# Two-layer decoder step on one core: more short products of ones ahead of the first block, the first norm's squares in another place and width, the end in two halves of tokens

## The chip, the core and the metric

The kernel runs on one core of a Trainium2 chip. A core has five engines with a queue of instructions each, and work on one waits for work on another by semaphores: TensorE (PE: matrix products, with a separate row PEld for loading weights), VectorE (DVE: elementwise work), ScalarE (ACT: elementwise functions with a scale), GpSimd (POOL: elementwise, and slower) and SyncE (SP: here it issues nearly all transfers between device memory and the on-chip memory). Sixteen DMA engines carry the transfers. Products land in PSUM, a small memory of banks from which DVE and ACT read.

The metric is the device time of one execution in microseconds. Before the change it is 601.29 us, the median of 3 runs (601.08 to 602.26). A separate execution was profiled; its time and span stand in the table below.

## The reference, cut to what matters

264 columns of tokens (256 of a prompt and 8 single tokens of a sample group) pass two layers of width 1024, a mixer and a feed-forward net each, and a final norm:

```python
def rmsnorm(x, g):
    xf = x.astype(jnp.float32)
    y = xf * lax.rsqrt(jnp.mean(xf * xf, axis=-1, keepdims=True) + EPS)
    return (y * g).astype(x.dtype)

def moba_gmlp_mixer(x, pos, past_kv, norm_g, w_in, sgu_gain, sgu_w, sgu_b, w_out):   # layer 0
    h = rmsnorm(x, norm_g)
    z = h @ w_in
    q, k, v, bu, bv = jnp.split(z, [...], axis=-1)
    ...                                   # rotary positions, attention, a gated mixer
    return x + y, new_kv, bvn
...
xp, cp = conv_ffn(xp, conv_zero, ffn_norm[layer], ...)      # after each mixer
y_prompt = rmsnorm(xp, final_norm)
y_sample = rmsnorm(xs, final_norm)
```

Two things of it matter here: the very first `rmsnorm` with the product `h @ w_in` behind it, and the very last `rmsnorm`, whose result is the output `y`.

## The kernel before, in words

**Layout.** The residual stream lies transposed: channels on the 128 partitions (eight groups `m` of 128), 264 tokens along the free dimension. A weight matrix is cut into blocks of 128x128; a block is one step of `run`, and eight blocks are a tile of weights. To keep float32 accuracy each weight tile and each operand is split into a high and a low part: ACT copies the high part (`wh`, `xg_h`), DVE subtracts it from the source (`wl`, `xg_l`), and a block is three products of PE: high x high, high x low, low x high (the order on PE is `xg_h,wh`, `xg_l,wh`, `xg_h,wl`). All of PE's products carry line L215 in the profile, since a helper issues them; they are told apart by the tiles' names.

**Blocks and tiles of the first product.** Layer 0's input product has 160 blocks. Blocks 0 to 19 run over the channel groups k = 0 to 4 with four outputs inside (the four parts of `bv`); blocks 20 to 31 finish these four with k = 5 to 7; from block 32 on each output takes eight blocks in a row (q, k, bu, v). Tile t is blocks 8t to 8t+7. Tiles 0 and 1 and the input x come in six packed transfers `xw`; tiles 2 to 5 in one transfer each (`raw2` to `raw5`, 512 KB), from `raw6` on two tiles to a transfer (1 MB; `raw6` holds tiles 6 and 7).

**The first norm.** The norm's factor R is one number per token, so the kernel multiplies x by the gain only and divides later: the products start before R is known, and R is applied where a result leaves PSUM (`in0_evac`). R needs the sum of the squares over all channels: ACT squares each of the eight groups (`Norm.add`, L399), POOL adds them up one by one (L408, L411), two products with a matrix of ones (`ns_n`, float32, each in two passes) add over partitions, and ACT takes Ln and Exp (L431, L432). Up to that point the results of blocks 0 to 31 are held in four PSUM banks. Then DVE computes the tables `rope` (L657 to L659) and evacuates `bv` (L695), q and k (L687 to L693). The first use of q and k on PE is the attention product `S` of the first two heads.

**What sets the order.** Early instructions are pinned with `tc.keep_in_program_order`; the rest of the queues is laid out by a scheduler when the program is built. `run` walks over the blocks; hooks (`blk(b, f)`) insert other work on PE after b blocks, and from the first hook on PE's order is the program's. Before: `blk(30, norm0)`, `blk(82, s_qk, 0)`, `blk(108, gm_var)`. SP's queue is in order: transfers, and between them reads of the page table into registers (`page_regs`, L340). Buffers come from pools; a pool called `up` has 24 slots of one size, taken in turn, and a new tile waits until its slot's last owner is done.

**Ahead of the first product** PE runs `WARM` = 12 products of a matrix of ones (256 columns, bf16) whose result nobody reads.

**The end.** The last matrix product adds its eight outputs into X (`residual(..., operand=False)`): DVE adds (L598), ACT squares (L399), POOL sums, ACT multiplies X by the final gain (L603). The last group's squares go into the sum as a second product of ones. After Ln and Exp, DVE multiplies X by R in five pieces of 1, 2, 2, 2 and 1 channel groups (`YD`, L1109), and SP and ACT in turn send each piece out (L1110).

Of the kernel before, what the change touches and what calls it, by code (L numbers as in the profile page):

```python
# [34 lines left out]

MMB = 4
KQ = 5
WARM = 12
YD = ((0, 1), (1, 3), (3, 5), (5, 7), (7, 8))

NEG = -1e30
SCALE = HD ** -0.5
# [108 lines left out]
def _consts():  # L151
# [41 lines left out]
    ("sguw", (P, 512)), ("sgub", (P, 512)), ("poolw", (P, 512)),  # L193
]
_OUTS = [
    ("y", (KD, P, T)), ("k0", (P, 4, T)), ("v0", (P, 4, T)), ("bvn", (P, 4, NS)),
    ("k1", (P, 4, T)), ("v1", (P, 4, T)), ("poolp", (P, 4, NST)), ("pools", (P, 4, NS, 16)),
    ("cv0", (P, NF, 10)), ("cv1", (P, NF, 10)), ("cs0", (P, NF, NS)), ("cs1", (P, NF, NS)),
]
# [3 lines left out]
def tile_decoder_step(ctx: ExitStack, tc: tile.TileContext, a):  # L203
# [36 lines left out]
    def at(name):  # L240
        return psa.tile([P, 512], F32, tag="at", name=name)
# [45 lines left out]

    LOOK = 3
    pos = [0]

    def split(t):
        for tt in range(len(splits), min(t + (2 if t == 3 else LOOK), NT - 1) + 1):
            ci = chunk_of[tt]
            for c in range(ci, min(ci + 3, len(_CHUNKS))):
                raw(c)
            o = (tt * 8 - coff[ci]) * P
            src = raws[ci][:, o:o + 8 * P]
            h, l = splits[tt] = wtiles(tt)
            s.activation(h, src, AF.Copy)  # L299
            v.tensor_tensor(l, src, h.bitcast(F32), ALU.subtract)  # L300
        return splits[t]

    spare = (32, 40)
# [65 lines left out]
    warm = con.tile([P, 256], BF16, name="warm")  # L369
    tc.keep_in_program_order(v.memset(warm, 1.0))  # L370
    pw = at("warm")
    for i in range(WARM):
        tc.keep_in_program_order(pe.matmul(pw[:, :256], warm[:, :P], warm, start=i == 0, stop=i == WARM - 1))

    ident = cst("ident")
    ones = con.tile([P, P], F32, name="ones")
# [13 lines left out]
            tc.keep_in_program_order(j)  # L390

    class Norm:
        def __init__(self, name, two=False):
            self.name, self.two, self.last = name, two, []
            self.acc = None

        def add(self, m, src=None):
            q = sm.tile([P, T], F32, tag="sq", name=f"sq_{self.name}{m}")
            i = s.activation(q, X[:, m, :] if src is None else src, AF.Square)  # L399
            if src is not None:  # L400
                tc.keep_in_program_order(i)
            if m == KD - 1 and self.two:
                self.last.append(q)
            elif self.acc is None:
                self.acc = q
            elif m == 1:
                n = sm.tile([P, T], F32, tag="acc", name=f"acc_{self.name}", bufs=2)
                g.tensor_tensor(n, self.acc, q, ALU.add)  # L408
                self.acc = n
            else:  # L410
                g.tensor_tensor(self.acc, self.acc, q, ALU.add)  # L411

        def finish(self, pin=False):
            return rstd_of([self.acc] + self.last, 1.0 / D, self.name, pin)
# [6 lines left out]
        def finish2(self):  # L421
# [127 lines left out]
    def ffn(l, xg, nrm, down_evac, hooks=None):  # L549
        cw, cb = vec("cw"), vec("cb")  # L550
        wc = lambda i, j: cw[:, (l * 3 + i) * NF + j:(l * 3 + i) * NF + j + 1]
        cvo = sm.tile([P, NF, 10], F32, tag="cvo", name=f"cvo{l}", bufs=1)
        act = [mv(f"a{l}_{i}") for i in range((NF + 3) // 4)]
        half = {}
        R = None
        nrm.split()

        def norm():
            nonlocal R
            R = nrm.finish2()  # L560
# [31 lines left out]
    def residual(gain, name, operand=True):  # L592
        xg = [mv(f"xg_{name}{i}") for i in range(2)] if operand else None
        nrm = Norm(name, not operand)

        def evac(m, o):
            m = m[1]
            v.tensor_tensor(X[:, m, :], X[:, m, :], o, ALU.add)  # L598
            if operand:
                operand_tile(xg[m // 4], m, X[:, m, :], gain[:, m:m + 1])  # L600
            nrm.add(m)
            if not operand:
                s.activation(X[:, m, :], X[:, m, :], AF.Copy, scale=gain[:, m:m + 1])  # L603
        return xg, nrm, evac

    def pick(xg):
        return lambda m, k: hl(xg, k)
# [3 lines left out]


    xg = [mv(f"xg_0{i}") for i in range(2)]
    nrm = Norm("n0", True)
    for tt in range(2):
        splits[tt] = wtiles(tt)

# [19 lines left out]
    for m in range(1, 5):  # L637
        part(m, s)()
        operand_tile(xg[m // 4], m, xin[m], GAIN[:, m:m + 1], pin=True)
        if m != 2:  # L640
            nrm.add((m - 1) // 2 if m < 4 else 2, xin[(m - 1) // 2 if m < 4 else 2])
    whole(2)
    for m in range(5, KD):
        operand_tile(xg[m // 4], m, xin[m], GAIN[:, m:m + 1], pin=True)
    for m in range(3, KD):
        nrm.add(m, xin[m])
        if m == 4:
            whole(3)
        elif m == 6:
            whole(4)  # L650
    rope = f4("rope")
    R0, held = [], []

    def norm0():
        R = nrm.finish(pin=True)
        R0.append(R)
        v.tensor_tensor(rope[:, 0, :], CS[:, 0, :], R, ALU.mult)  # L657
        v.scalar_tensor_tensor(rope[:, 2, :], CS[:, 1, :], SCALE, R, ALU.mult, ALU.mult)
# [285 lines left out]
    st1 = {}  # L944

    qz1 = sample_z("l1")

    def norm1():
        nonlocal R
        R = nrm1.finish2()  # L950
        sigmoid_set()

    edge = f4("edge", (P, 384))
# [150 lines left out]
    _, nrm, evac = residual(vec("fin"), "fin", operand=False)  # L1104
    ffn(1, xg, norm_f, evac)
    R = nrm.finish()
    for i, (m, e) in enumerate(YD):
        x = X[:, m:e, :]
        v.tensor_tensor(x, x, R.unsqueeze(1).to_broadcast([P, e - m, T]), ALU.mult)  # L1109
        (s if i % 2 else nc.sync).dma_start(a["y"][m:e].rearrange("m p t -> p m t"), x)  # L1110


def _lay(inp):
# [66 lines left out]
```

## Time and profile before

| what | before |
|---|---|
| device time, median of 3 runs | 601.29 us (601.08 to 602.26) |
| device time of the profiled execution | 602.49 us |
| span of the profiled execution | 600.7 us |
| PE busy | 588.6 us, 98% of the span |
| DVE busy | 422.9 us, 70% |
| ACT busy | 343.3 us, 57% |
| POOL busy | 107.9 us, 18% |
| first and last block product starts on PE | 5.08 us, 591.30 us |

A row of the timeline reads: start in us from the span's start, duration in us, engine, line, operation, what is written <- what is read, shape, count; in brackets how long the engine was idle before and what it waited for. Rows with a count above one merge neighbours of the same kind. In the table of windows each engine has its busy time in the stretch. The profiled execution took 1.8 us more than its span. PE is busy nearly all the time, so the places where it is not, at both ends and in between, are few and can be listed.

### The profile page before, as it was taken

The page shows a single profiled execution, that of the slowest core. Times are in us where ns is not written, and L with a number is a line of the kernel's source. Part 1 is how long each engine was busy: PE and PEld are TensorE (multiplying, and loading weights), DVE is VectorE, ACT ScalarE, POOL GpSimd, SP SyncE. Part 2 cuts the span into 40 slices and gives each one's busy share as a digit, 9 for nine tenths or more (in the row PEclk, how much of TensorE's full clock was granted, in tenths as well). Part 3 has the DMA queues.
Part 4 walks back from the last instruction along what each step waited for, and adds up shares of the span by engine and source line. Part 5 has one row for each costly group of instructions (what it writes and reads, how often), then busy time and mean ns, then how long its engine had stood idle before and what let it go on. Part 6 is the DMA issues. An engine that isn't in the chain of part 4 may idle for free.

```text
span 600.7 us, 12394 instructions
## 1 busy us (share of the span) xinstructions
PE 588.6 (98%) x4900; PEld 569.6 (95%) x4900; DVE 422.9 (70%) x733; ACT 343.3 (57%) x600; POOL 107.9 (18%) x103
## 2 busy tenths in 40 slices
PE   8999999999999999999999999999999999999994
PEld 6988879999999999999999879999999999999994
DVE  7899565977778777665559676687777777864432
ACT  7657754675655656644454466657656565564441
POOL 4100002303222232210120000031232323211110
PEclk9999999999999999999999999999999999999998
DMA  8998835454555545795467763554545454555402
GB/s 319 337 399 323 316 121 202 152 201 152 200 170 182 186 165 202 264 378 214 155 247 256 261 203 113 174 204 148 201 154 206 147 205 159 193 187 202 181 1 74
DMA packets 28092, 122.42 MB, mean 204 GB/s; under 512 B 3330, under 2 KB 5250, under 8 KB 16642
## 3 DMA queue, kind: packets, MB, share of 16 engines
q1 hardware_dynamic: 27200, 120.42, 56.1%
q10 hardware_dynamic: 834, 1.20, 0.6%
q8 instruction: 39, 0.64, 0.4%
q14 instruction: 19, 0.16, 0.1%
HBM read 117.65 MB, written 3.96 MB: 202 GB/s over the span
## 4 chain that ended last, share of the span: by engine, by line
PE 92%; DVE 3%; DMA 2%; SPq 1%; issue 1%; ACT 0%; ACTq 0%; DVEq 0%
PE mm L215 85%; DMA raw<-in_w 1%; PE pv_l L215 1%; PE sc L215 1%; DVE wl L300 1%; PE pav L215 1%; PE pt L218 1%; DMA PT<-in_pt 1%; PE S L215 1%; SPq L340 1%; PE Z L215 1%; PE pf L215 0%; DVE X L1109 0%; PE pm L215 0%; DVE rz_q L687 0%
## 5 line engine op out<-in xcount | busy, mean ns | idle before, releaser
L300 DVE TENSOR_TENSOR wl<-raw,wh 128x1024 fp32r<-128x1024 f32 x179 | 218.9, 1224 | 78.1 <-ACT wh L299 77.9
L299 ACT ACTIVATE wh<-raw 128x1024 fp32r<-128x1024 f32 x179 | 188.6, 1055 | 92.7 <-PE mm L215 84.1
L215 PE MATMUL mm<-xg_f_h,wh 128*128 128x264 f32 x704 | 200.1, 284 | 0.0
L215 PE MATMUL mm<-xg_f_l,wh 128*128 128x264 f32 x704 | 199.9, 284 | 0.0
L215 PE MATMUL mm<-xg_f_h,wl 128*128 128x264 f32 x704 | 198.6, 282 | 0.0
L215 PEld LDWEIGHTS mm<-xg_f_l,wh 128*128 128x128 f32 x704 | 132.3, 188 | 0.0
L215 PEld LDWEIGHTS mm<-xg_f_h,wh 128*128 128x128 f32 x704 | 132.2, 188 | 0.0
L215 PEld LDWEIGHTS mm<-xg_f_h,wl 128*128 128x128 f32 x704 | 132.2, 188 | 0.0
L582 POOL TENSOR_TENSOR wk<-wk 128x264 f32<-128x264 f32 x44 | 66.5, 1513 | 193.9 <-DVE wk L581 159.3
L215 PE MATMUL mm<-a_h,wh 128*128 128x264 f32 x352 | 100.1, 284 | 0.0
L215 PE MATMUL mm<-a_l,wh 128*128 128x264 f32 x352 | 99.9, 284 | 0.0
L215 PE MATMUL mm<-a_h,wl 128*128 128x264 f32 x352 | 99.4, 282 | 0.0
L215 PEld LDWEIGHTS mm<-a_l,wh 128*128 128x128 f32 x352 | 66.1, 188 | 0.0
L215 PEld LDWEIGHTS mm<-a_h,wh 128*128 128x128 f32 x352 | 66.1, 188 | 0.0
L215 PEld LDWEIGHTS mm<-a_h,wl 128*128 128x128 f32 x352 | 66.1, 188 | 0.0
L442 ACT ACTIVATE a_h<-wk 128x264 fp32r<-128x264 f32 x44 | 18.7, 424 | 73.3 <-POOL wk L582 73.3
L215 PE MATMUL mm<-xg_h,wh 128*128 128x264 f32 x160 | 47.5, 297 | 1.1 <-ACT xg_h L386 1.1
L443 DVE TENSOR_TENSOR a_l<-wk,a_h 128x264 fp32r<-128x264 f32 x44 | 19.2, 437 | 41.5 <-ACT a_h L442 41.5
L215 PE MATMUL mm<-xg_h,wl 128*128 128x264 f32 x160 | 45.7, 285 | 0.7 <-DVE wl L632 0.6
L215 PE MATMUL mm<-xg_l,wh 128*128 128x264 f32 x160 | 45.6, 285 | 0.1
L215 PE MATMUL mm<-xg_n_h,wh 128*128 128x264 f32 x128 | 38.4, 300 | 0.0
L215 PE MATMUL mm<-xg_n_l,wh 128*128 128x264 f32 x128 | 36.3, 283 | 0.0
(245 smaller groups left out, 897.3 us busy)
## 6 DMA issues: line engine op xcount, KB each, us to landing
raw<-in_w SPq DMA_DIRECT2D x89, 1024.0 KB, 4.8
K<-in_kt SPq DMA_DIRECT2D x32, 256.0 KB, 6.7
V<-in_vp SPq DMA_DIRECT2D x32, 256.0 KB, 5.2
raw<-in_w SPq DMA_DIRECT2D x4, 512.0 KB, 5.7
X<-in_x SPq DMA_DIRECT2D x4, 264.0 KB, 6.4
xw<-in_xw SPq DMA_DIRECT2D x2, 388.0 KB, 5.5
out_k<-k SPq DMA_DIRECT2D x1, 528.0 KB
out_v<-v SPq DMA_DIRECT2D x1, 528.0 KB, 5.0
```

Source lines behind the costliest of these rows:

```text
L215: return self.keep(nc.tensor.matmul(*x, **k))
L218: return self.keep(nc.tensor.transpose(*x, **k))
L299: s.activation(h, src, AF.Copy)
L300: v.tensor_tensor(l, src, h.bitcast(F32), ALU.subtract)
L340: regs.append(nc.sync.value_load(PT[0:1, i:i + 1], min_val=0, max_val=NPHYS - 1))
L442: s.activation(h, src, AF.Copy)
L443: v.tensor_tensor(l, src, h.bitcast(F32), ALU.subtract)
L582: g.tensor_tensor(A, A, C, ALU.mult)
```

## The change

Five edits:

1. `WARM` goes from 12 to 18 products, and one more of 128 columns (`busy(128)`) stands inside block 0, between its second and third product.
2. The first norm's squares leave their places among the first splits. ACT now squares groups 0 to 3 after the split of tile 3 and groups 4 and 5 to 7 (the latter three in one instruction, 128x792) after that of tile 4. POOL adds the first four (128x528, then 128x264), DVE adds the other four the same way and then both sums (`sum0`). One product of ones takes the place of two. The hook moves from block 30 to block 34, and so behind the splits of tiles 5, 6 and 7.
3. SP issues `raw6` before the reads of the page table and before `CST`; `VEC` moves to a hook at block 64.
4. Hooks further on move: `s_qk` from blocks 82 and 95 to 86 and 97, `gm_var` from 108 to 113.
5. The end works on two halves of 132 tokens: the last group is added and squared in halves, the product of ones over it and Ln and Exp are done per half, DVE writes two new tiles `y0` and `y1` (seven instructions instead of five; the last channel group takes its gain there, so ACT's L603 falls away for it), and five transfers of 4+4 and 4+2+2 groups send them out. `y` in device memory becomes (2, 128, 8, 132); the host transposes it.

```diff
-WARM = 12
-YD = ((0, 1), (1, 3), (3, 5), (5, 7), (7, 8))
+WARM = 18
+TH = T // 2
...
             pe.matmul(o, h[:, c:c + P], xl, start=False, stop=False)
+            if i == 0:
+                busy(128)
             pe.matmul(o, l[:, c:c + P], xh, start=False, stop=left[m] == 0)
...
     raw(5)
+    raw(6)
     page_regs(4)
     late(CST, a["cst"])
-    raw(6)
-    page_regs(4)
-    late(VEC, a["vec"])
-    page_regs(4)
+    page_regs(8)
...
-        if m != 2:
-            nrm.add((m - 1) // 2 if m < 4 else 2, xin[(m - 1) // 2 if m < 4 else 2])
     whole(2)
...
-    for m in range(3, KD):
-        nrm.add(m, xin[m])
-        if m == 4:
-            whole(3)
-        elif m == 6:
-            whole(4)
+    whole(3)
+    sq0 = [f4(f"sq0_{i}") for i in range(2)]
+    def sum0(e, q):
+        keep(e.tensor_tensor(q[:, 0:2, :], q[:, 0:2, :], q[:, 2:4, :], ALU.add))
+        keep(e.tensor_tensor(q[:, 0, :], q[:, 0, :], q[:, 1, :], ALU.add))
+    for m in range(4):
+        keep(s.activation(sq0[0][:, m, :], xin[m], AF.Square))
+    sum0(g, sq0[0])
+    whole(4)
+    keep(s.activation(sq0[1][:, 0, :], xin[4], AF.Square))
+    keep(s.activation(sq0[1][:, 1:4, :], first[5][2], AF.Square))
+    sum0(v, sq0[1])
+    summed = keep(v.tensor_tensor(sq0[1][:, 0, :], sq0[0][:, 0, :], sq0[1][:, 0, :], ALU.add))
...
-        R = nrm.finish(pin=True)
+        R = rstd_of([sq0[1][:, 0, :]], 1.0 / D, "n0", True)
...
-    blk(30, norm0)
+    blk(34, norm0)
+    blk(64, late, VEC, a["vec"])
-    for t, b in enumerate((82, 95, 108, 121)):
+    for t, b in enumerate((86, 97, 108, 121)):
         blk(b, s_qk, t)
-    blk(108, gm_var)
+    blk(113, gm_var)
...
+            for c in halves_:
+                keep(v.tensor_tensor(X[:, m, c], X[:, m, c], o[:, c], ALU.add))
+                keep(s.activation(sq[:, c], X[:, m, c], AF.Square))
+        def rest():
+            keep(pe.matmul(p[:, :T], ones, nrm.acc, start=True, stop=False, skip_group_check=True))
+            for c in halves_:
+                keep(pe.matmul(p[:, c], ones, sq[:, c], start=False, stop=True, skip_group_check=True))
+            ...
+            for i, c in enumerate(halves_):
+                Y = f4(f"y{i}", (P, KD, TH))
+                cuts = ((0, 4), (4, 8)) if i == 0 else ((0, 4), (4, 6), (6, 8))
+                for n, (m, e) in enumerate(cuts):
+                    w = min(e, KD - 1)
+                    keep(v.tensor_tensor(Y[:, m:w, :], X[:, m:w, c], R[:, c].unsqueeze(1).to_broadcast([P, w - m, TH]), ALU.mult))
+                    if e == KD:
+                        keep(v.scalar_tensor_tensor(Y[:, w, :], X[:, w, c], gain[:, w:w + 1], R[:, c], ALU.mult, ALU.mult))
+                    (s if n % 2 else nc.sync).dma_start(a["y"][i][:, m:e, :], Y[:, m:e, :])
```

In `split`, two hints of order to the scheduler are added: tile 5's low part behind the last sum, and a hint for tiles below 8 that are split after R, of which there are none with the hook at block 34.

More of the change, by code (lines that the diff above doesn't have):

```diff
@@ L289, in tile_decoder_step @@
     pos = [0]
+    R0 = []
     def split(t):
@@ L298, in split @@
             h, l = splits[tt] = wtiles(tt)
-            s.activation(h, src, AF.Copy)
-            v.tensor_tensor(l, src, h.bitcast(F32), ALU.subtract)
+            i = s.activation(h, src, AF.Copy)
+            if R0 and tt < 8:
+                behind(i, last[0])
+            i = v.tensor_tensor(l, src, h.bitcast(F32), ALU.subtract)
+            if tt == 5:
+                behind(i, summed)
         return splits[t]
@@ L371, in tile_decoder_step, with busy @@
     pw = at("warm")
+    def busy(n):
+        tc.keep_in_program_order(pe.matmul(pw[:, :n], warm[:, :P], warm[:, :n], start=True, stop=True))
     for i in range(WARM):
-        tc.keep_in_program_order(pe.matmul(pw[:, :256], warm[:, :P], warm, start=i == 0, stop=i == WARM - 1))
+        busy(256)
     ident = cst("ident")
@@ L392, in tile_decoder_step, with __init__, add @@
     class Norm:
[L393 to L397, printed above, removed]
+        def __init__(self, name):
+            self.name, self.acc = name, None
+        def add(self, m):
             q = sm.tile([P, T], F32, tag="sq", name=f"sq_{self.name}{m}")
[L399 to L404, printed above, removed]
+            s.activation(q, X[:, m, :], AF.Square)
+            if self.acc is None:
                 self.acc = q
@@ L411, in add @@
                 g.tensor_tensor(self.acc, self.acc, q, ALU.add)
-        def finish(self, pin=False):
-            return rstd_of([self.acc] + self.last, 1.0 / D, self.name, pin)
         def split(self):
@@ L419, in split, with finish @@
             halves(*self.hl, self.acc)
-        def finish2(self):
+        def finish(self):
             return rstd_of(self.hl, 1.0 / D, self.name, w=onesr)
@@ L559, in norm @@
             nonlocal R
-            R = nrm.finish2()
+            R = nrm.finish()
             gelu_set()
@@ L590, in ffn, with residual @@
         run(orders[f"dn{l}"], lambda m, k: hl(act, k), down_evac, hooks)
-    def residual(gain, name, operand=True):
-        xg = [mv(f"xg_{name}{i}") for i in range(2)] if operand else None
-        nrm = Norm(name, not operand)
+    def residual(gain, name):
+        xg = [mv(f"xg_{name}{i}") for i in range(2)]
+        nrm = Norm(name)
         def evac(m, o):
@@ L598, in evac, with final, rstd @@
             v.tensor_tensor(X[:, m, :], X[:, m, :], o, ALU.add)
-            if operand:
-                operand_tile(xg[m // 4], m, X[:, m, :], gain[:, m:m + 1])
+            operand_tile(xg[m // 4], m, X[:, m, :], gain[:, m:m + 1])
             nrm.add(m)
-            if not operand:
-                s.activation(X[:, m, :], X[:, m, :], AF.Copy, scale=gain[:, m:m + 1])
-        return xg, nrm, evac
+        return xg, nrm, evac
+    def final():
+        nrm = Norm("fin")
+        gain = vec("fin")
+        halves_ = [slice(0, TH), slice(TH, T)]
+        sq = sm.tile([P, T], F32, tag="R", name="sq_last", bufs=2)
+        keep = tc.keep_in_program_order
+        def evac(m, o):
+            m = m[1]
+            if m < KD - 1:
+                v.tensor_tensor(X[:, m, :], X[:, m, :], o, ALU.add)
+                nrm.add(m)
+                s.activation(X[:, m, :], X[:, m, :], AF.Copy, scale=gain[:, m:m + 1])
+                return
+            for c in halves_:
+                keep(v.tensor_tensor(X[:, m, c], X[:, m, c], o[:, c], ALU.add))
+                keep(s.activation(sq[:, c], X[:, m, c], AF.Square))
+        def rest():
+            p = at("ns_fin")
+            R = sm.tile([P, T], F32, tag="R", name="R_fin", bufs=2)
+            keep(pe.matmul(p[:, :T], ones, nrm.acc, start=True, stop=False, skip_group_check=True))
+            for c in halves_:
+                keep(pe.matmul(p[:, c], ones, sq[:, c], start=False, stop=True, skip_group_check=True))
+            def rstd(c):
+                keep(s.activation(R[:, c], p[:, c], AF.Ln, bias=epst, scale=1.0 / D))
+                keep(s.activation(R[:, c], R[:, c], AF.Exp, scale=-0.5))
+            for c in halves_:
+                rstd(c)
+            for i, c in enumerate(halves_):
[7 more added lines that the diff above has]
+                    (s if n % 2 else nc.sync).dma_start(a["y"][i][:, m:e, :], Y[:, m:e, :])
+        return evac, rest
@@ L946, in tile_decoder_step @@
     qz1 = sample_z("l1")
+    R = None
     def norm1():
         nonlocal R
-        R = nrm1.finish2()
+        R = nrm1.finish()
         sigmoid_set()
@@ L1103, in tile_decoder_step @@
     norm_f = nrm
-    _, nrm, evac = residual(vec("fin"), "fin", operand=False)
+    evac, rest = final()
     ffn(1, xg, norm_f, evac)
[L1106 to L1110, printed above, removed]
+    rest()
 def _lay(inp):
@@ L1159 @@
     o = {n: np.asarray(r.results[0]["out_" + n]) for n, _ in _OUTS}
-    y = o["y"].transpose(2, 0, 1).reshape(T, D)
+    y = o["y"].transpose(0, 3, 2, 1).reshape(T, D)
     def kv(k, w):
```

6 lines of the change are left out of this document (3 added, 3 removed).

## The prediction

> **What bounds the kernel now.** I read the page's busy line, the list of what PE waited for, and then the timeline at both ends.
>
> ```profile
> span 600.7 us, 12394 instructions
> PE 588.6 (98%) x4900; PEld 569.6 (95%) x4900; DVE 422.9 (70%) x733; ACT 343.3 (57%) x600; POOL 107.9 (18%) x103
> PE mm L215 <- ACT xg_h L386: 1.1, 1, 1.1
> PE mm L215 <- DVE wl L632: 0.6, 1, 0.6
> ```
>
> PE is the bound from 40 us to the last product; there it has no wait at all. Gains can come only from the first 40 us and from what follows the last product. The list counts only waits of half a microsecond and more, so I price PE by the times at which blocks start. Of the rows below, 7.94 is the first product of block 5, 18.32 the first norm product (30 blocks done), 19.57 the first of block 31, 38.11 the first mask product of S (82 blocks done).
>
> ```profile
> 1.20 2.74 PE L215 MATMUL warm<-warm 128*128 128x256 bf16 x12 [1.20 <-DVE warm L370]
> 5.08 0.39 PE L215 MATMUL mm<-xg_h,wh 128*128 128x264 f32 x1 [1.15 <-ACT xg_h L386]
> 5.61 0.19 PEld L215 LDWEIGHTS mm<-xg_l,wh 128*128 128x128 f32 x1 [0.34 <-DVE xg_l L387]
> ...
> 7.72 0.39 PE L215 MATMUL mm<-xg_h,wl 128*128 128x264 f32 x1
> 7.94 0.28 PE L215 MATMUL mm<-xg_h,wh 128*128 128x264 f32 x1
> ...
> 18.32 0.61 PE L215 MATMUL ns_n<-acc_n,ones 128*128 128x264 f32 x2
> ...
> 19.57 0.29 PE L215 MATMUL mm<-xg_h,wh 128*128 128x264 f32 x1
> ...
> 38.11 0.39 PE L215 MATMUL S<-maskb,identb 128*128 128x256 bf16 x2
> 39.49 0.93 PE L215 MATMUL S<-k,q 64*128 64x128 f32 x8 [0.99 <-DVE k L693]
> ```
>
> Blocks 31 to 81 take 18.54 us, 0.3635 each, with no stall. Blocks 5 to 29 would take 9.09 at that pace and took 10.38: **1.29 us lost** to waits for DVE. From 18.32 to 19.57 lie one block and the two norm products: 0.89, so 0.445 a product. S's two mask products take 0.22 (the second runs 0.11 behind the first), so 38.33 was due and 39.49 came: **1.16 lost**.
>
> Why DVE is late:
>
> ```profile
> 8.59 0.48 DVE L387 SCALAR_TENSOR_TENSOR xg_l<-xw,xw,xg_h 128x264 fp32r<-128x264 f32 x1
> 10.16 0.98 DVE L387 SCALAR_TENSOR_TENSOR xg_l<-xw,xw,xg_h 128x264 fp32r<-128x264 f32 x1
> 12.20 2.30 DVE L387 SCALAR_TENSOR_TENSOR xg_l<-xw,xw,xg_h 128x264 fp32r<-128x264 f32 x3
> 14.43 3.47 DVE L632 TENSOR_TENSOR wl<-raw,wh 128x1024 fp32r<-128x1024 f32 x2
> 17.82 1.21 DVE L300 TENSOR_TENSOR wl<-raw,wh 128x1024 fp32r<-128x1024 f32 x1
> 9.98 0.87 POOL L411 TENSOR_TENSOR acc_n<-acc_n,sq_n 128x264 f32<-128x264 f32 x1 [0.29 <-ACT sq_n L399]
> 12.46 4.35 POOL L411 TENSOR_TENSOR acc_n<-acc_n,sq_n 128x264 f32<-128x264 f32 x4 [1.61 <-ACT sq_n L399]
> ```
>
> The same `xg_l` takes 0.48 alone and 0.98 beside a POOL add; `wl` 1.21 alone and about 1.77 beside one. Over these rows that is about 2.5 us of DVE time.
>
> The chain of waits up to the tables `rope`:
>
> ```profile
> 12.82 7.99 DMA raw<-in_w
> 20.91 1.06 ACT L299 ACTIVATE wh<-raw 128x1024 fp32r<-128x1024 f32 x1 [4.50 <-DMA raw<-in_w]
> 22.37 0.43 ACT L432 ACTIVATE R_n<-R_n 128x264 f32<-128x264 f32 x1
> 23.15 0.43 DVE L657 TENSOR_TENSOR rope<-ropecs,R_n 128x264 f32<-128x264 f32 x1
> 39.01 0.43 DVE L693 TENSOR_TENSOR k<-k,rz_k 128x264 f32<-128x264 f32 x1
> ```
>
> R's sum was ready near 19.3, but on ACT's queue Ln stands behind tile 6's split, which waited for `raw6` until 20.9. From 23.15 to 39.44 DVE works without a gap, and its `k` is what S waits for.
>
> **The change, part by part.**
>
> *Products of ones.* Twelve took 2.74, 0.22 apart, so six more end near 5.2, at most 0.15 after PE's first block could start. Block 0's second product waits 0.34 for `xg_l` anyway and its third for `wl`; the 128-column product (0.06 to 0.11) fits before the third. Cost 0, between +0.3 (all of it on the path) and -0.3 (the clock is up sooner). If that cover were gone, it would be 0.15.
>
> *Squares on ACT.* The next start behind each row gives ACT's pace: an `xg_h` 0.41, a square 0.31, a split 0.95.
>
> ```profile
> 10.69 1.32 ACT L386 ACTIVATE xg_h<-xw,xw 128x264 fp32r<-128x264 f32 x3
> 11.91 0.72 ACT L399 ACTIVATE sq_n<-xw 128x264 f32<-128x264 f32 x2
> 12.53 1.05 ACT L631 ACTIVATE wh<-raw 128x1024 fp32r<-128x1024 f32 x1
> 13.48 0.72 ACT L399 ACTIVATE sq_n<-xw 128x264 f32<-128x264 f32 x2
> ```
>
> Tile 2's split began at 9.74, behind two squares that no transfer hid; now it starts at about 9.1 and tile 3's at 11.35. Four squares run from 12.3 to 13.55, tile 4's split to 14.5, the squares of groups 4 to 7 to 15.6 (the wide one 0.75, by its width between a square and a split), tile 5's split to 16.5.
>
> *Sums.* POOL now starts at 13.6 instead of before 9.98, so DVE runs undisturbed until then: tile 2's `wl` ends by 11.4, the three `xg_l` by 12.6, tile 3's `wl` by 13.7. PE, unstalled, asks for them at block 16 (11.94), block 20 (13.4) and block 24 (14.85). All 1.29 us go. Next comes tile 4's `wl` at 14.55: even at 1.77 it is done by 16.35, and block 32 is at 17.75. DVE's three adds (0.62, 0.35, 0.35 by its 528- and 264-column rows below) end near 17.7. That is new work on DVE and the thinnest place: the norm product is due at 18.48 (block 34). Tile 5's `wl` then ends by 18.9, wanted at 21.1 (block 40).
>
> The Trainium skill, page "SBUF — State Buffer", section "Who interferes with whom", says that DVE with two inputs in this memory and a reading GpSimd instruction exclude each other for the whole instruction. The rows agree that beside POOL an instruction is longer by half of one of POOL's. By that rule they would take turns: POOL's wide add to 15.5 (twice its 0.87 and more), `wl` to 16.7, POOL's second to 17.6, DVE's adds to 18.9, and PE would wait 0.45: an estimate, and the forecast would be 598.4.
>
> *One norm product instead of two*: 0.445 less on PE.
>
> *`raw6` earlier.* SP issues it behind `raw5` (9.70 + 0.43) instead of at 12.82:
>
> ```profile
> 9.70 0.43 SPq L274 DMA_DIRECT2D raw<-in_w  x1
> 18.17 0.33 SPq L274 DMA_DIRECT2D raw<-in_w  x1
> DMA to landing us min/median/max: 4.9/7.1/9.0
> ```
>
> By the `raw` transfers of the first 45 us it lands between 15.0 and 19.1; I take 17.7, near the median. Tile 6's split then ends at 18.75, tile 7's at 19.7 (PE frees its buffer at block 32), Exp at 20.7. DVE has `wl` of tiles 6 and 7 to 21.15, then `rope`: 2.0 sooner than 23.15, with tile 7 (1.14, which stood between `bv` and q) already done. `CST`, passed by 1 MB, lands some 3 us later than it would, before the masks need it at 21. The next `raw`, at 18.17, moves by less than 0.4, since SP's sixteen reads stay. `VEC` is wanted at block 130 and costs nothing at block 64.
>
> *S at block 86.* Its `k` is ready at 21.15 + (39.44 - 23.15) - 1.14 = 36.3. PE reaches block 86 at 7.94 + 81 x 0.3635 + 0.445 = 37.83, and S proper at 38.05. No wait; 1.16 goes, with 1.7 us to spare. With `raw6` at 19.1 `rope` would come at 22.4 and S would still not wait. The banks of `bv` are the other limit: block 48 (24.0) takes the first one, emptied some 1.45 after `rope` begins, at 22.6.
>
> *Hooks.* Moved work is the same work. `gm_var` comes at block 113 instead of 108; 17 blocks, 6.2 us at 0.3635, stay for its chain before block 130, where its result is wanted. I cost this at nothing; each microsecond that the chain lacks would cost one.
>
> Early sum: 1.29 + 0.445 + 1.16 = **2.89 us**.
>
> *The end.*
>
> ```profile
> 591.62 0.43 DVE L598 TENSOR_TENSOR X<-X,mm 128x264 f32<-128x264 f32 x1 [7.56 <-PE mm L215]
> 594.33 2.63 DVE L1109 TENSOR_TENSOR X<-X,R_fin 128x264 f32<-128x264 f32 x5 [2.29 <-ACT R_fin L432]
> L1109 DVE TENSOR_TENSOR X<-X,R_fin 128x528 f32<-128x528 f32 x3 | 1.9, 700 | 0.0
> L1109 DVE TENSOR_TENSOR X<-X,R_fin 128x264 f32<-128x264 f32 x2 | 0.9, 430 | 2.3 <-ACT R_fin L432 2.3
> 597.50:598.50 1.00, 0.00 (x0) 0.50 1.04 362
> 8.00:10.00 2.00, 1.00 1.04 414
> ```
>
> From the add to DVE's first multiplication: 2.71 us. In the built program the second Ln has no wait of its own, so the first waits for the products of both halves. The second half of the add ends 0.08 later (one more seam), its square, Ln and Exp each lose about 0.1 (between none and half of some 0.42), the product 0.22: 2.27, or 0.44 sooner. DVE's seven pieces: 1.02 ns a column from the two rows, so 0.70 + 0.565 + 0.295 + 0.70 + 0.43 + 2 x 0.295 = 3.28, less six seams of 0.083 = 2.78 against 2.63. The last transfer is issued 0.29 sooner, the first, twice as large, 0.17 sooner. The DMA engines are full at 362 GB/s (the windows show it); pieces with twice the bytes in a row could go at up to 414, another 0.5. I take 0.4, between 0.17 and 0.8.
>
> Sum: 2.89 + 0.4 = 3.3 us. Against the profiled execution 602.49 - 3.3 = 599.2; the median of the runs shown is 1.2 lower, so **598.0 us**.
>
> **The rivals.**
> - *R is late all the same.* If `raw6` still lands at 20.9, Ln stands behind two splits and `rope` comes at 23.85; block 48 waits for its bank until 25.25, 1.25 us. Gain 2.0: 599.3. For it: a transfer's landing is not set by its issue alone, 12.82 took 7.99. Against: none took over 9.0.
> - *DVE stays the bound.* If POOL is not what stretches DVE, 1.8 of the 2.5 us fall before tile 3's `wl`, which PE then awaits for about 0.9, and the rest makes the norm product some 0.5 late. Gain 2.89 - 1.4 + 0.4 = 1.9: 599.4, and past 600.1 if the new adds are stretched too. The rows with and without a POOL add speak against it.
> - *The clock comes up later.* The ones ran 0.22 apart and the mask products, as wide, 0.11: PE began at half speed. If it stayed there through blocks 1 to 4, twelve products would take 0.12 longer each, 1.4, of which block 4 hides some 0.2, since its product at 7.72 waits that long already: 599.2. The Trainium skill, page "TensorE: Matmul & The Clock Gate", section "What's actually happening", gives a free-running window of about 3.4 us that must be busy; six more products fill it, so by that rule the change makes this rarer.
> - *Slower.*
>
> ```profile
> 50.51 0.35 SPq L896 DMA_DIRECT2D out_k<-k  x1
> 63.17 0.82 PE L218 MATMUL pt<-CST,p 128*128 128x128 f32 x6
> ```
>
> Two new tiles shift the turn of `up`: the transposes' copy of heads 2 and 3 now takes the slot of `k`, which the transfer `out_k` reads (issued at 50.51). PE needs that copy at block 129 (the second row), 2.89 sooner than before: 60.3. At 9.0 to landing the copy is done at 60.4; each microsecond beyond costs one, and only from 13.7 on is the kernel slower by 0.2%. No transfer shown takes that long: 602.6.
>
> **How the numbers follow.** Forecast 0.70 (own range 597.2 to 598.6), late R 0.10, DVE 0.08, clock 0.06, slower 0.06. The range 597.0 to 599.9 takes in the bounds of the end and all but the last case and the worse half of DVE's. About 0.2%, 1.2 us, can be told from no change, so faster means under 600.1: 0.88; the same 0.06 (half of the DVE case, and milder forms of the last); slower 0.06.
>
> **What would show it.** Right: `xg_l` near 0.48 and `wl` near 1.21 before 14 us, no PE wait at L632, the norm product near 18.5, `rope` near 21.2, S without a wait near 38, the last group's add some 2.9 us earlier than 591.62, and about 8.7 us from it to the end of the span instead of 9.1. Wrong: a PE wait for `sq` at the norm product, for `bv` at block 48, or for `k` at S.

## The result, and the profile after

| what | before | after |
|---|---|---|
| device time, median of 6 executions each | 601.39 us (601.08 to 602.62) | 599.26 us (598.98 to 599.47) |
| ratio | | 0.9956, 95% interval 0.9945 to 0.9967 |
| device time of the profiled execution | 602.49 us | 599.23 us |
| span of the profiled execution | 600.7 us | 597.2 us |

The kernel became faster by 2.1 us, 0.44%. The forecast was 598.0 (597.0 to 599.9), 3.3 us of gain: the direction and the range held, the gain forecast was half as large again as the one measured, and the narrower range that the prediction gave its own case (597.2 to 598.6) was missed. The two profiled executions, however, lie 3.26 apart.

The page's busy line and PE's timeline of the changed kernel; the columns are those of the prediction's rows:

```profile
span 597.2 us, 12397 instructions
PE 588.4 (99%) x4907; PEld 570.4 (96%) x4907; DVE 423.4 (71%) x739; ACT 342.5 (57%) x600; POOL 104.8 (18%) x99
```

```profile
1.20 4.02 PE L215 MATMUL warm<-warm 128*128 128x256 bf16 x18 [1.20 <-DVE warm L375]
4.87 0.47 PE L215 MATMUL mm<-xg_h,wh 128*128 128x264 f32 x1
...
7.63 0.39 PE L215 MATMUL mm<-xg_h,wl 128*128 128x264 f32 x1 [0.21 <-DVE wl L666]
7.86 0.28 PE L215 MATMUL mm<-xg_h,wh 128*128 128x264 f32 x1
...
18.39 0.61 PE L215 MATMUL ns_n<-sq,ones 128*128 128x264 f32 x2
...
37.74 0.39 PE L215 MATMUL S<-maskb,identb 128*128 128x256 bf16 x2
38.06 0.93 PE L215 MATMUL S<-k,q 64*128 64x128 f32 x8
```

Block 5 starts at 7.86, the norm product behind block 33 at 18.39: 29 blocks in 10.53, 0.363 each, so no stall is left between them. S runs behind its mask products without a wait.

DVE, POOL and ACT of the same execution:

```profile
9.51 0.49 DVE L397 SCALAR_TENSOR_TENSOR xg_l<-xw,xw,xg_h 128x264 fp32r<-128x264 f32 x1
12.45 1.22 DVE L674 TENSOR_TENSOR wl<-raw,wh 128x1024 fp32r<-128x1024 f32 x1
14.47 1.52 DVE L674 TENSOR_TENSOR wl<-raw,wh 128x1024 fp32r<-128x1024 f32 x1 [0.80 <-ACT wh L673]
15.92 1.25 DVE L691 TENSOR_TENSOR sq<-sq 128x528 f32<-128x528 f32 x1
17.21 0.43 DVE L692 TENSOR_TENSOR sq<-sq 128x264 f32<-128x264 f32 x1
17.75 0.43 DVE L701 TENSOR_TENSOR sq<-sq,sq 128x264 f32<-128x264 f32 x1
...
21.63 0.42 DVE L708 TENSOR_TENSOR rope<-ropecs,R_n 128x264 f32<-128x264 f32 x1
13.57 1.35 POOL L691 TENSOR_TENSOR sq<-sq 128x528 f32<-128x528 f32 x1 [11.13 <-ACT sq L695]
14.99 1.62 POOL L692 TENSOR_TENSOR sq<-sq 128x264 f32<-128x264 f32 x1
18.26 2.01 ACT L300 ACTIVATE wh<-raw 128x1024 fp32r<-128x1024 f32 x2 [1.54 <-DVE sq L701]
```

Ahead of POOL's start at 13.57 DVE's instructions have their short durations (0.49, 1.22); the last sum ends at 18.18, 0.2 ahead of the product that wants it. Tiles 6 and 7 are split from 18.26 on, where tile 6 had begun at 20.91, and `rope` comes at 21.63 instead of 23.15. The last row names DVE's sum as what ended ACT's wait, since it ended last; by the trace's record `raw6` landed at 18.16, and in all ten profiles with `raw6` in the new place this split begins 0.1 behind its landing.

The end, in the timeline and in the view by windows (mean clock, share of the DMA engines and GB/s stand last):

```profile
588.74 0.49 DVE L622 TENSOR_TENSOR X<-X,mm 128x132 f32<-128x132 f32 x2 [7.56 <-PE mm L215]
590.93 1.19 DVE L643 TENSOR_TENSOR y<-X,R_fin 128x528 f32<-128x528 f32 x2 [1.70 <-ACT R_fin L634]
590.19 0.37 ACT L633 ACTIVATE R_fin<-ns_fin,epst 128x132 f32<-128x132 f32 x1 [0.60 <-PE ns_fin L215]
591.67 2.52 SPq L646 DMA_DIRECT2D out_y<-y  x3
594.00:594.50 0.50, 0.00 (x0) 0.00 (x0) 0.00 (x0) 0.00 (x0) 0.00 (x0) 0.50 1.00 368
```

The last group's add starts 2.88 sooner than before, and from it to the span's end (597.17 unrounded, 600.72 before) it takes 8.43 where it took 9.10: 0.67 less. The first transfer is issued 2.93 behind the add where it was 3.18 (594.79 in the kernel before): 0.25 sooner. The other 0.42 lies in the stream itself. In its second half microsecond the old stream, whose first piece is one channel group, falls to 131 GB/s, the new one to 292 (first row before, second row after):

```profile
596.00:596.50 0.50, 0.00 (x0) 0.00 (x0) 0.50 (x2) 0.00 (x0) 0.00 (x0) 0.50 0.39 131
593.00:593.50 0.50, 0.00 (x0) 0.00 (x0) 0.50 (x4) 0.00 (x0) 0.00 (x0) 0.50 0.81 292
```

### The profile page after: what moved, and what is told of

It is laid out like the page before. It is cut to its first block, busy times and chain, and to the rows that moved or that the text cites. A ratio compares the mean times of both kernels' runs of the same rounds, so it can differ in the third digit from the quotient of the medians.

```text
span 597.2 us, 12397 instructions
## 1 busy us (share of the span) xinstructions
PE 588.4 (99%) x4907; PEld 570.4 (96%) x4907; DVE 423.4 (71%) x739; ACT 342.5 (57%) x600; POOL 104.8 (18%) x99
## 4 chain that ended last, share of the span: by engine, by line
PE 97%; DMA 1%; DVE 1%; ACT 0%; DVEq 0%; issue 0%; SPq 0%
PE mm L215 90%; PE pv_l L215 1%; PE sc L215 1%; PE pav L215 1%; PE pt L218 1%; DMA xw<-in_xw 1%; PE S L215 1%; PE Z L215 1%; PE pf L215 0%; DVE y L643 0%; PE pm L215 0%; PE vtp_v L218 0%; PE po_l L218 0%; PE vtp_sgu L218 0%; PE ns_fin L215 0%; DVE wl L666 0%
## 5 line engine op out<-in xcount | busy, mean ns | idle before, releaser
L215 PE MATMUL mm<-xg_n_l,wh 128*128 128x264 f32 x128 | 36.3, 284 | 0.0
```

The lines of the kernel that those rows point to most:

```text
L215: return self.keep(nc.tensor.matmul(*x, **k))
```

## The experiments

Three theories stood at the start, on why 3.3 in the profiles was 2.1 in the medians. **A**: S's wait of 1.16 for `k` stands only in some executions of the kernel before, the profiled one among them. **B**: every execution has it, and the changed kernel loses a microsecond where its profile shows nothing. **C**: the scatter comes from the start. From the fifth run on A is told as theory R: `raw6` lands at different times, and R with all that follows it. Each comparison's own "before" runs on the same chip as the kernels beside it, so medians of different comparisons aren't set against each other.

**The kernel before, again** (no edit).

> The kernel before, unchanged. Theory A: the 1.16 us wait of S for k, counted as a loss of every execution, stands only in some of them, the profiled one of 602.49 among them; then the executions fall near 601.2 (span near 599.4) and near 602.4 (span near 600.6), and a profile with the short span shows S's first product of k and q without a wait, near 38.3 instead of 39.49. Rival B: the wait is in every execution and the changed kernel loses about 1.1 us in a place that its profile doesn't show; then every profile of this kernel has S near 39.5. Rival C: the scatter sits at the start (transfers of x, clock), so that the short span has its block 5 near 6.8 instead of 7.94 and still waits 1.16 for k.

Measured: 602.48 median of 12 (601.35 to 603.53), and 602.11 for the 32 executions of the same kernel that served as its base (601.18 to 606.50; three of them lie above 605, for a reason that no profile shows). The profile, of an execution of 602.34, has the wait again:

```profile
39.35 0.93 PE L215 MATMUL S<-k,q 64*128 64x128 f32 x8 [1.04 <-DVE k L693]
22.47 0.43 DVE L657 TENSOR_TENSOR rope<-ropecs,R_n 128x264 f32<-128x264 f32 x1
30.89 1.23 DVE L300 TENSOR_TENSOR wl<-raw,wh 128x1024 fp32r<-128x1024 f32 x1 [0.41 <-ACT wh L299]
```

R came sooner here: `rope` starts at 22.47, 0.68 ahead of the first profile, and yet S starts only 0.14 sooner. DVE lost the rest at 30.89, where it waited 0.41 for a later tile's split; on ACT's queue that split stands behind the split of tile 8, whose transfer had landed late too (split at 25.02 instead of 24.70). So R and the transfers behind `raw6` both set when `k` is ready.

On this chip the typical execution of the kernel before is 0.7 longer than the first median said, and but for those three the times spread evenly rather than in two groups. Both profiles of this kernel, at 602.34 and 602.49, have the wait. No profile of an execution near 601.2 is on record, so that the wait is missing there stays an inference.

**S later, in the kernel before.**

```diff
-    for t, b in enumerate((82, 95, 108, 121)):
+    for t, b in enumerate((86, 97, 108, 121)):
```

> The kernel before with S of heads 0 to 3 at blocks 86 and 97 instead of 82 and 95, nothing else. Theory A: the median stays near 601.3, since most executions have no wait to lose, but the ones near 602.4 are gone (none over 601.8). Rival B: 1.16 less in all, 600.2. Rival C: the same median and the same scatter as before, 601.0 to 602.6.

Measured: 602.15 (601.41 to 603.41) against 602.11: ratio 0.9994, interval 0.9974 to 1.0013. A and B both missed; C's forecast, the same median and the same scatter, came nearest. The profile is of the shortest execution, 601.41; rows of PE:

```profile
4.78 0.59 PE L215 MATMUL mm<-xg_h,wh 128*128 128x264 f32 x1 [0.84 <-ACT xg_h L386]
...
7.79 0.42 PE L215 MATMUL mm<-xg_h,wl 128*128 128x264 f32 x1
8.01 0.34 PE L215 MATMUL mm<-xg_h,wh 128*128 128x264 f32 x1
...
17.98 0.61 PE L215 MATMUL ns_n<-acc_n,ones 128*128 128x264 f32 x2
...
51.94 0.49 PE L215 MATMUL pmu<-bsum,ones 128*128 128x264 f32 x1 [0.23 <-DVE bsum L804]
```

S no longer waits, but the next product that needs DVE's work does: the mean of `bsum` at block 100, by 0.23. In this execution Exp of R stood at 21.34, a microsecond sooner than the 22.37 of the first profile; had it been as late, `pmu` would have waited some 1.2 (an estimate from these rows). So what is late is DVE's whole queue behind R, and moving one consumer hands the wait to the next. The rows up to 8.01 are 0.22 apart: PE was still at half speed, and yet the norm product came at 17.98, no later than the 18.32 of the first profile. DVE is the bound up to there, and the late clock cost nothing that shows at the norm product of this execution.

**The old squares in the changed kernel**: ACT's eight squares in their old places, POOL's six adds and two products of ones as before, the hook still at block 34.

```diff
...
-        R = rstd_of([sq0[1][:, 0, :]], 1.0 / D, "n0", True)
+        R = rstd_of(acc0 + sq7, 1.0 / D, "n0", True)
...
```

> The changed kernel with the first norm's squares, sums and two products of ones of the kernel before (the hook stays at block 34). By the sum of the prediction 1.29 + 0.445 = 1.73 us come back: 599.26 + 1.73 = 601.0 in theory A and rival B alike; xg_l takes 0.98 and wl 1.77 again before 18 us. If DVE's lateness was not worth what the blocks' times say, about 599.7 (the product of ones alone).

Measured: 600.72 (600.52 to 601.04), profiled 600.70. The stall is back at the same place, and the last group's add moves from 588.74 to 590.50, 1.76 later, against the sum's 1.73:

```profile
16.20 0.39 PE L215 MATMUL mm<-xg_h,wl 128*128 128x264 f32 x1 [0.59 <-DVE wl L672]
19.70 0.61 PE L215 MATMUL ns_n<-acc_n,ones 128*128 128x264 f32 x2
590.50 0.49 DVE L620 TENSOR_TENSOR X<-X,mm 128x132 f32<-128x132 f32 x2 [7.56 <-PE mm L215]
```

Of the 1.76, 1.31 stands already at the first norm product (19.70 against 18.39), which is the term of DVE; the remaining 0.45 is the second product. Both terms are real, and beside POOL's adds `xg_l` takes 0.98 and `wl` 1.77 again. The span grew by as much, the time of the profiled executions by 1.47 only: 0.3 lies outside the span (last section).

**The old end in the changed kernel**: one R of full width, five pieces.

> The changed kernel with the old end (full-width R, five pieces of 1, 2, 2, 2, 1 groups). Prediction: 0.4 (0.17 to 0.8) comes back, 599.7; by the two profiles 9.08 against 8.46 from the last group's add to the span's end, 0.62: 599.9. If the end scatters as much as that, 599.3.

Measured: 600.07 median of 9 (599.65 to 601.04). Its profile, of the longest execution, shows something beside the end: tile 6 was split only at 20.00, and PE waited for the bank of `bv`.

```profile
20.00 2.01 ACT L300 ACTIVATE wh<-raw 128x1024 fp32r<-128x1024 f32 x2 [2.87 <-DMA raw<-in_w]
24.97 0.36 PE L215 MATMUL mm<-xg_h,wh 128*128 128x264 f32 x1 [0.69 <-DVE bv L727]
589.88 0.43 DVE L613 TENSOR_TENSOR X<-X,mm 128x264 f32<-128x264 f32 x1 [7.56 <-PE mm L215]
```

From the add to the span's end (598.98) it takes 9.10 again, so the new end is worth 0.67 in the profile. That the add itself starts 1.14 later than in the changed kernel's profile belongs to the start, where the two kernels are the same (1.11 of it is there when S starts, at 39.17 against 38.06): the prediction's "late R" does happen, in a part of the executions. The changed kernel didn't run beside this one, so the medians don't price the end.

**The changed kernel, again**, in a comparison of its own with the next three.

> The changed kernel, unchanged, beside the kernel before on one chip. Theory R (the landing of raw6 differs from execution to execution; R, the banks of bv and S's k follow it; the kernel before waits for them more or less, the changed one hardly): 599.3 with a range under 0.6, and before near 602.1 as in the last comparison, so 2.8 apart rather than 2.1. Rival C (the scatter is the time at which the clock comes up): the changed kernel scatters by 0.5 to 1 as well when more executions are seen.

Measured: 599.86 (599.31 to 601.24) against 602.47: 0.9953, interval 0.9941 to 0.9965. The base and the distance of 2.6 are near theory R's, the median is 0.6 over its 599.3, and the range of 1.9 is C's. Its profile is of the execution of 601.24:

```profile
5.36 0.59 PE L215 MATMUL mm<-xg_h,wh 128*128 128x264 f32 x1
...
10.03 0.42 PE L215 MATMUL mm<-xg_h,wh 128*128 128x264 f32 x1
10.25 0.37 PE L215 MATMUL mm<-xg_l,wh 128*128 128x264 f32 x1
10.46 0.29 PE L215 MATMUL mm<-xg_h,wl 128*128 128x264 f32 x1
10.58 0.28 PE L215 MATMUL mm<-xg_h,wh 128*128 128x264 f32 x1
...
20.39 0.61 PE L215 MATMUL ns_n<-sq,ones 128*128 128x264 f32 x2
```

The spacing falls from 0.22 to 0.12 only at 10.46. The norm product comes 2.0 later than at 18.39, the span is 2.0 longer, and PE has no wait listed behind its first product: most of it is the clock. A part is the start: the first product comes 0.49 later than at 4.87, since ACT waited for x until 4.79 instead of 4.16.

**`raw6` late, in the changed kernel.**

```diff
     raw(5)
-    raw(6)
     page_regs(4)
     late(CST, a["cst"])
+    raw(6)
```

> The changed kernel with raw6 issued where the kernel before issues it, behind four reads of the page table and CST. Theory R: raw6 lands 2 or more later, tiles 6 and 7 are split near 21 and R comes near 23, PE waits for the bank of bv at block 48 (0.7 to 1.5): median 600.0 to 600.8, range over 0.8. Rival C: 599.3, and as tight as the changed kernel.

Measured: 600.75 (599.89 to 600.98), 0.9 over the changed kernel beside it. With six executions each, whose ranges overlap, the times alone don't tell the two apart; the profile, of 600.98, shows what theory R forecast, with a longer wait:

```profile
20.61 2.01 ACT L300 ACTIVATE wh<-raw 128x1024 fp32r<-128x1024 f32 x2 [4.33 <-DMA raw<-in_w]
25.58 0.36 PE L215 MATMUL mm<-xg_h,wh 128*128 128x264 f32 x1 [1.66 <-DVE bv L746]
```

**Twelve products of ones in the changed kernel**, and none inside block 0.

> The changed kernel with 12 products of ones and without the one in block 0. By the prediction (cost and gain 0): 599.3. Rival C: with the gap ahead of block 0 the clock comes up later in a part of the executions, median 599.3 to 600.0 and single ones up to 1.4 above the lowest.

Measured: 600.21 (599.23 to 600.87), against 599.86: not told apart. In its profile, of 600.60, the spacing falls to 0.12 at 9.56. A late clock is thus seen with 12 and with 18 products; whether it is rarer with 18 stays open.

**`raw6` early, in the kernel before.**

```diff
     raw(5)
+    raw(6)
     page_regs(4)
     late(CST, a["cst"])
-    raw(6)
```

> The kernel before with raw6 ahead of the reads of the page table and of CST, nothing else. Theory R: R comes near 21, S at block 82 doesn't wait for k, the losses of DVE (1.29) and the second product of ones (0.445) are no longer covered by that wait and stay: 601.2 with a range under 0.8. Rival C: the scatter from 601.2 to 603 stays.

Measured: 601.41 median of 12 (601.24 to 602.26) against 602.47: 0.9983, interval 0.9975 to 0.9992. This one move takes a microsecond off and most of the scatter with it; C, by which the scatter would have stayed, falls for this kernel. The profile, of 601.34:

```profile
18.98 1.06 ACT L299 ACTIVATE wh<-raw 128x1024 fp32r<-128x1024 f32 x1 [1.13 <-DVE wl L300]
...
16.17 0.39 PE L215 MATMUL mm<-xg_h,wl 128*128 128x264 f32 x1 [0.58 <-DVE wl L632]
...
38.32 0.93 PE L215 MATMUL S<-k,q 64*128 64x128 f32 x8
...
590.46 0.43 DVE L598 TENSOR_TENSOR X<-X,mm 128x264 f32<-128x264 f32 x1 [7.56 <-PE mm L215]
```

S starts at 38.32 without a wait (38.33 was the prediction's due time), while DVE's early stalls are still there. The last group's add starts 1.16 sooner than in the first profile (591.62), which is S's wait, and 1.72 later than in the changed kernel's (588.74), which is the other two terms of the early sum. Over all profiles tile 6's split begins at 19.88 to 20.91 in the four with `raw6` in the old place, and at 17.96 to 20.00 in the ten with it in the new one.

**Filling block 0's waits, another end, and both**, beside the changed kernel once more.

```diff
             pe.matmul(o, h[:, c:c + P], xh, start=first, stop=False)
+            if i == 0:
+                busy(256)
             pe.matmul(o, h[:, c:c + P], xl, start=False, stop=False)
             if i == 0:
+                busy(192)
+            pe.matmul(o, l[:, c:c + P], xh, start=False, stop=left[m] == 0)
+            if i == 0:
                 busy(128)
-            pe.matmul(o, l[:, c:c + P], xh, start=False, stop=left[m] == 0)
```

```diff
-            for c in halves_:
-                keep(pe.matmul(p[:, c], ones, sq[:, c], start=False, stop=True, skip_group_check=True))
...
             for c in halves_:
+                keep(pe.matmul(p[:, c], ones, sq[:, c], start=False, stop=True, skip_group_check=True))
                 rstd(c)
...
-                cuts = ((0, 4), (4, 8)) if i == 0 else ((0, 4), (4, 6), (6, 8))
+                cuts = ((0, 2), (2, 5), (5, 8)) if i == 0 else ((0, 4), (4, 6), (6, 8))
```

> The changed kernel, unchanged, as the base of the three beside it: 599.3 in executions whose clock is up by 5.1 us, up to 2 more in those whose clock comes up later (10.4 in the profile of 601.24); median 599.3 to 599.9.

> The changed kernel with block 0's waits filled: products of ones of 256 columns behind its first product, 192 behind its second, 128 behind its third. Theory P (the clock record moves in steps of 3.41 us and goes up at the end of a step in which PE was busy for about 0.78 or more; the steps that failed so far had 0.71 to 0.76 of it and held block 0's waits or the gap ahead of it): the step that holds block 0 now passes in every execution, the clock is up by 7.3 at the latest, no execution is over 1.2 above the lowest, median 599.1 to 599.5. Rival: the scatter has another source; then the median and the range are those of the changed kernel, and if the added products stand on the path the lowest goes up by 0.1 to 0.3.

> The changed kernel with another end: Ln and Exp of the first half issued ahead of the second half's product, so that its Ln needn't wait for that product, and the first half sent in pieces of 2, 3 and 3 groups instead of 4 and 4. If the start of the DMA stream sets the end: Ln starts 0.35 sooner, the first piece is ready another 0.25 sooner, and from the last group's add to the span's end it takes 7.9 instead of 8.46: 0.5 to 0.6 off the changed kernel's median. If the last piece sets it, at most 0.35; if Ln still waits for both products, 0.25 or less.

> Both edits in one: 598.5 to 598.9 if both theories hold, and no execution over 1.2 above the lowest; 599.3 if neither does.

Measured, 5 executions each: the changed kernel 599.24 (598.93 to 599.43), filled 599.50 (599.05 to 600.23), the other end 598.99 (598.76 to 599.09), both 598.92 (598.60 to 599.79), against 602.0 of the kernel before. No late clock was seen in these profiles, in the changed kernel neither, so theory P isn't tested; the filled kernel's profile has a wait of 0.38 for `bv` instead (tile 6 at 19.46). The other end, in its timeline:

```profile
588.78 0.49 DVE L622 TENSOR_TENSOR X<-X,mm 128x132 f32<-128x132 f32 x2 [7.56 <-PE mm L215]
590.00 0.37 ACT L630 ACTIVATE R_fin<-ns_fin,epst 128x132 f32<-128x132 f32 x1 [0.38 <-PE ns_fin L215]
590.96 0.37 ACT L630 ACTIVATE R_fin<-ns_fin,epst 128x132 f32<-128x132 f32 x1 [0.24 <-PE ns_fin L215]
590.43 0.49 PE L215 MATMUL ns_fin<-sq_last,ones 128*128 128x132 f32 x2 [0.46 <-ACT R_fin L630]
591.21 2.86 SPq L644 DMA_DIRECT2D out_y<-y  x4
```

The first transfer is issued 2.43 behind the add instead of 2.93, the span (596.93) ends 8.15 behind it instead of 8.43. Half a microsecond at the stream's start became 0.3 at its end, and the first Ln came only 0.23 sooner: the second half's product now waits 0.46 for that Ln, which reads the same PSUM tile. The median is 0.25 below the changed kernel's, within a spread of 0.3 to 0.5; it is the better version by its trace, and by its times only as far as five executions tell.

## Why the prediction was right, and where it was not

**The sum for the profiled execution was right.** "Early sum: 1.29 + 0.445 + 1.16 = 2.89 us": the last group's add came 2.88 sooner. Term by term: the norm product was forecast for 18.48 and came at 18.39, S for 38.05 and came at 38.06, and the old squares put back cost 1.76 for the two terms' 1.73. The forecast against the profiled execution, 599.2, stands beside 599.23; that it is as close as this is luck, since 0.29 of the 3.55 by which the span fell didn't reach the device time, and the end gave 0.27 more than was taken for it.

**The step that failed is the last one of the sum: "the median of the runs shown is 1.2 lower, so 598.0 us".** It took all three losses from a median to which the third doesn't belong in full. S's wait hangs on when `raw6` and the transfers behind it land, and that differs between executions; the profile came from a long one, and the 1.2 by which it lay over the median was of the size of the very wait to be removed. `raw6` issued sooner in the kernel before shows it: 601.4, hardly any scatter, no wait of S, the other two losses in place. Without S's wait the sum is 1.29 + 0.445 + 0.67 - 0.21 (time outside the span) = 2.2, about the distance of the medians of 2.1.

That most executions of the first comparison lacked the wait is inferred; the profile with `raw6` early shows what such an execution looks like, and its span is 2.40 longer than the changed kernel's, against 1.29 + 0.445 + 0.67 = 2.41. The times bear this out less cleanly: beside each other on one chip these two kernels lie 1.55 apart in their medians and 1.93 in their shortest executions, with the late clock in at least one of the changed kernel's. The hidden loss of theory B was found in no profile. In the two comparisons where the kernel before had 602.5 and 602.0, the distance was 2.6 and 2.8.

**That the stated range held owes something to luck.** The prediction gave 0.70 to its own case, 597.2 to 598.6, and 599.26 lies outside it. It lies inside 597.0 to 599.9 because that range took in the rivals, whose times of 599.2 to 599.4 are near the measured one; none of their mechanisms is in the profiled execution.

**The thinnest place held, barely.** The sums were forecast to end near 17.7, ended at 18.18, and were wanted at 18.39. The sum of the forecast left POOL's second add out: the 528-column add, priced at 0.62, took 1.25 beside it. The rows fit turns, where an instruction's recorded time holds its wait. `wl`, 1.22 alone, started at 14.47 beside POOL's first add, which ended at 14.92, and ended at 15.99 (16.14 by turns); POOL's second add ended 0.62 behind it, at 16.61; the wide add ended at 17.17 (17.23 by turns). That is the rule of the Trainium skill's page "SBUF — State Buffer", section "Who interferes with whom", and the trace agrees within 0.15. The prediction's estimate by it, 18.9, came out late because POOL was priced too dear: it took the wide POOL add to end at 15.5, from twice 0.87. That 0.87, at 9.98, held a wait for DVE in its turn, for a `wl` that ended at 10.24, and the add ended 0.61 behind that:

```profile
9.14 1.10 DVE L624 TENSOR_TENSOR wl<-xw,wh 128x512 fp32r<-128x512 f32 x1
```

The prediction's reading of the rows, that DVE is longer by half of one of POOL's, goes with it: `xg_l` and `wl` were longer by 0.50 and 0.56, nearly all of the 0.6 that a POOL add takes behind the DVE instruction beside it.

**`raw6` and R** came about as taken: the split at 18.26 (17.8 by the sum), `rope` at 21.63 (21.15). `k` was ready at 37.23 instead of 36.3, so S had 0.8 to spare and not 1.7. The rival "R is late all the same" had 0.10; it is a share of the executions rather than a case: waits for `bv` of 0.69 and 0.38 stand in two of nine profiles that have the changed kernel's order of transfers.

**The end** gave 0.67, inside the bounds of 0.17 and 0.8. DVE's first multiplication came 2.19 behind the add (2.27 by the sum). The first transfer went 0.25 sooner (0.17 by the sum), the last 0.31 (0.29). What did not come is a higher full rate: the stream with twice the bytes in a row moved at 368 GB/s where the old one moved at 362. What came in its place is a fuller start of the stream, 292 GB/s where the old one fell to 131.

**The products of ones** were costed at nothing, and no run shows a cost or a gain clear of the scatter. The rival "the clock comes up later" was priced at 1.2 on the ground that the clock is up by block 4; in one execution it wasn't before 10.46, and cost 2.0. That the change makes this rarer has no support in these runs.

**Slower** did not happen: the transposes at block 129 ran at 60.28, and no wait stands ahead of them.

## What to carry to other kernels

Before a loss read from one profile is taken off a median, see whether that profiled execution lies on the median: a wait that ends with a transfer's landing differs from execution to execution, and may itself be the distance. Two waits in a row on one late queue are one loss, so moving the first consumer away hands the wait to the next one (S, then `pmu`); it is the source that has to move, here one transfer ahead of a few register reads. Where two engines take turns, a recorded duration can hold a wait, and it is the end that counts and not the duration. An engine that no longer waits for another can show what that wait had covered, here the clock's late rise.

## What the runs showed of the hardware

- **The clock rises in steps that the kernel doesn't set.** The record of the granted clock in the fourteen traces has a full-speed stretch of 583.68, 587.09 or 590.51 us in every one, so 3.41 apart; it began between 3.9 and 10.4 us into the span, with 12 products as with 18. The Trainium skill, page "TensorE: Matmul & The Clock Gate", section "What's actually happening", gives a free-running window of about 3.4 us, with which these lengths agree. Its words "run-variable" are what the forecast left out: 18 products fill 3.9 us, and hold a whole window only if that happens to begin in their first half microsecond. What share of a window must be busy isn't settled here. The column of the clock in the view by windows reads 1.00 in the first microseconds even where products run 0.22 apart; the spacing of the products is what shows it there.
- **Some time lies outside the span, and an edit moved it.** Device time less span is 1.72 to 1.91 us in every execution of the five runs and their bases with single squares, and 1.92 to 2.10 in the nine runs with the wide ones (means about 1.79 and 2.00). That is 0.2 us that no view shows, with a cause that stays open.
- **The full rate of the output stream doesn't depend on these pieces**: 362 GB/s with 1056 bytes in a row, 368 in a stream where most rows have 2112. What the pieces change is how soon the stream is full.
- **POOL and DVE took turns in these rows**: a DVE instruction of 1.22 that started beside a POOL add took 1.52, and one of 0.48 took 0.98; each ended within 0.2 of the POOL add's end plus its own short time.
